# A hybrid retention and RG-LRU layer on one core: the order of instructions planned from a draft of the program, instead of by priorities

## The chip, the cores and the metric

The kernel runs on one core of a Trainium2 chip. The metric is the time of one execution on the device in microseconds (us), the median over several runs. Engines are named as in the profile: PE is TensorE (PEld its weight loads), DVE is VectorE, ACT is ScalarE, POOL is GpSimd, SP is SyncE, which here issues nearly all DMAs. Each engine takes its instructions in the one order that was fixed when the program was built.

## What is computed

One layer of a streaming encoder on 1024 positions of width 1024, in float32. The reference, cut to what matters here:

```python
h = rms_norm(x, norm1_w[l])
proj = h @ w_in[l]
q, k, v, g_ret, x_lru, y_lru, gate_ret, gate_lru = jnp.split(proj, SPLIT_POINTS, axis=-1)
...
o = chunkwise_retention(q, k, v.reshape(bsz, seq, RET_HEADS, RET_DV))
o = head_group_norm(o, ret_gn_w[l])
y_a = (o * jax.nn.silu(g_ret.astype(jnp.float32))).astype(x.dtype) @ w_ret_o[l]
xc = causal_depthwise_conv(x_lru, lru_conv_w[l], lru_conv_b[l])
hl = rg_lru(xc, lru_w_r[l], lru_b_r[l], lru_w_i[l], lru_b_i[l], lru_lambda[l])
y_b = (hl * jax.nn.gelu(y_lru.astype(jnp.float32))).astype(x.dtype) @ w_lru_o[l]
mix = (jax.nn.sigmoid(gate_ret + merge_gate_b[l, 0]) * y_a
       + jax.nn.sigmoid(gate_lru + merge_gate_b[l, 1]) * y_b)
x = x + mix @ w_out[l]
h = rms_norm(x, norm2_w[l])
up = h @ ffn_w_up[l]
gate, val = jnp.split(up, [D_FF], axis=-1)
gate = causal_depthwise_conv(gate, ffn_conv_w[l], ffn_conv_b[l])
x = x + (jax.nn.gelu(gate) * val) @ ffn_w_down[l]
return rms_norm(x, norm_f_w)
```

## The kernel before

**Matrix products.** Every large product is done in fp32r with a split of both operands into a high part and a rest: `split` copies a tile to fp32r on ACT (a CAST) and subtracts it on DVE, and three matmuls (`PASSES`) stand for one product. A `Job` is one piece of weights (256 columns, or 128 and 128) against all positions; its four weight blocks come by DMA (`loads`), and are split ahead (`preps`, driven by `pump`). Most jobs are `fast`: `mm_fast` does one level of Strassen's scheme, seven products of twelve matmuls instead of eight. It holds its sums in three PSUM banks; `keep` copies a bank to SBUF on ACT, `total` adds a bank to such a copy on DVE, and the bank is then used for another product. A late `keep` or `total` therefore stops PE at the next matmul into that bank. The right-hand operands are split into `hi` and `lo` by `operand`, `tsets` and `kept_sums`, generators that `build` drives between products.

**Buffers.** `Units` hands out numbered buffers of 128x512: `u` (81 in SBUF, for operands and everything else), `w` (22 in SBUF, for weights), `g` (6 PSUM banks for the large products) and `a` (2 PSUM banks for all small work). A name such as `g5_461` is bank 5 in its 461st use.

**Stages.** The jobs of the input projection come first (0 to about 770 us); `retention_head`, `ret_out` and `lru_block` run between them as generators that `advance` steps. In the retention (about 150 to 430 us) each block has three small steps that depend on each other: a product of 128 columns, a DVE multiplication with a mask, and products of 256 columns. In `lru_block` (about 440 to 720 us) a convolution on DVE and ACT gives two tiles, which are split; for each of two gates and two halves six small matmuls go to one of the two `a` banks, and an ACT sigmoid empties it. Then come the output projections of both branches, `w_out`, the norm, the up projection (about 970 to 1380 us) and three parts of the down projection, whose last one writes the output.

**What sets the order.** The Tile layer schedules the traced program by priorities: an instruction's place in the source sets its priority, and `tc.high_priority(offset)` moves it forward. `hp()` wraps the weight splits, `SOON` (400) the operand builders, `NOW` (3000) the copies and sums that empty a bank and what a job emits, and `OLD` (800) the last steps of the up projection. `Tap` records the last instruction of DVE and ACT, and `Behind` adds an edge without a semaphore, so that the operand splits that are issued through `BS` and `BV` do not stand before the last bank copy on their engine. As `Tap` and `Behind` issue the instructions, most DVE and ACT work has line L136 (`Tap`) or L153 (`Behind`) in the profile.

Of the kernel before, what the change touches and what calls it, by code (L numbers as in the profile page):

```python
# [125 lines left out]
class Tap:  # L126


    def __init__(self, eng):
        self.eng, self.last = eng, None  # L130

    def __getattr__(self, name):
        fn = getattr(self.eng, name)

        def call(*args, **kw):
            ins = fn(*args, **kw)  # L136
            self.last = ins.ins.name
            return ins
        return call


class Behind:


    def __init__(self, tc, eng):
        self.tc, self.eng, self.last = tc, eng, None
        self.how = mybir.DependencyInfo(mybir.DependencyClass.NoSync, mybir.DependencyReason.DATA)

    def __getattr__(self, name):
        fn = getattr(self.eng, name)  # L150

        def call(*args, **kw):
            ins = fn(*args, **kw)  # L153
            if self.last is not None:
                self.tc.add_manual_dep(ins.ins, self.last, self.how, reason="behind the banks' copies")
            return ins
        return call
# [12 lines left out]
NOW, SOON, OLD = 3000, 400, 800  # L170
# [10 lines left out]
def tile_trunk_layer(ctx, tc, x, xt, positions, params, consts, normf, w_in, w_ro, w_lo,  # L181
                     w_out, w_up, w_dn, w_gate, out):
    nc = tc.nc
    V, S, G, PE, SY = Tap(nc.vector), Tap(nc.scalar), nc.gpsimd, nc.tensor, nc.sync
# [32 lines left out]
    def hp(offset=1500):  # L217
        return tc.high_priority(offset=offset)

    def split(src, get=get, S=S, V=V):  # L220

        hi, lo = get(F32R), get(F32R)
        S.copy(hi, src)
        V.tensor_sub(lo, src, hi.bitcast(F32))
        return hi, lo

    BS, BV = Behind(tc, nc.scalar), Behind(tc, nc.vector)
# [28 lines left out]
    state = {"load": None, "prep": None, "blocks": 0, "raws": 0, "hp": False, "ff": 0, "reserve": RESERVE, "force": False}  # L258
# [77 lines left out]
    def pump(force=None):  # L336
        with (hp() if state["hp"] else nullcontext()):
            while force is not None and force[1] not in force[0].blk:
                assert next(state["prep"]) is not None
            while state["blocks"] < NBLK and len(W) >= 4:  # L340
                if next(state["prep"]) is None:
                    break
            while state["raws"] < AHEAD and len(W) >= 4 and W.free():
# [56 lines left out]
    def emit(jb, m, h, src, unit):  # L400
# [4 lines left out]
        if V.last != v:  # L405
            BV.last = V.last
# [1248 lines left out]
```

## Time and profile before

| what | value |
|---|---|
| median of 3 runs | 1633.09 us (1632.9 to 1635.78) |
| the profiled execution | 1634.66 us, its span (first to last instruction) 1632.8 us |
| granted TensorE clock, mean | 0.998 |
| busy DVE, ACT, POOL | 1322.2, 908.7, 46.3 us |
| bytes moved by DMA | 271.09 MB, 166 GB/s over the span |

In a row of the timeline the first number is the start in us from the start of the span, the second the time from the start of the row's first instruction to the end of its last. Brackets hold the idle time of that engine before the row and what ended it. In a row of windows stand the stretch and its length, and then the busy time of each engine with the number of instructions that began in it. A matmul is counted as busy to its modelled end, and matmuls overlap, so their spacing is less than their mean duration.

### The profile page before, as it was taken

How to read it: one execution, taken by the hardware profiler on the slowest of the kernel's cores; microseconds unless marked ns; L12 is line 12 of the kernel's file. 1: busy time of each engine (PE TensorE's matmuls, PEld its weight loads, DVE VectorE, ACT ScalarE, POOL GpSimd, SP SyncE). 2: the span in 40 equal slices, each digit the busy share in tenths (PEclk: the TensorE clock that was granted, in tenths of full speed). 3: DMA queues.
4: the chain of work that ended last, by engine and by line, in shares of the span. 5: the costliest groups of instructions: out<-in, count | busy, mean ns of one | idle time of the engine just before them, and what ended most of it. 6: DMA issues, size and time to landing. Idle time of an engine off the chain costs nothing.

```text
span 1632.8 us, 21508 instructions
## 1 busy us (share of the span) xinstructions
PE 1611.5 (99%) x7176; PEld 1317.7 (81%) x7176; DVE 1322.2 (81%) x2393; ACT 908.7 (56%) x1535; POOL 46.3 (3%) x68
## 2 busy tenths in 40 slices
PE   9999999999999999999999999999999999999998
PEld 7788888888887878778878778888888888888876
DVE  8998768686888888968879799777777778887885
ACT  7574544435477879863345675444444446463653
POOL 0001000000000000000000001000000000000000
PEclk9999999999999999999999999999999999999999
DMA  8253324142433437667797335444444456877751
GB/s 294 71 181 103 114 74 142 52 136 68 136 113 104 136 97 243 225 202 246 246 300 257 106 123 194 135 136 136 136 141 142 149 167 214 292 252 260 258 191 67
DMA packets 151439, 271.09 MB, mean 166 GB/s; under 512 B 16800, under 2 KB 25120, under 8 KB 151328
## 3 DMA queue, kind: packets, MB, share of 16 engines
q1 hardware_dynamic: 145664, 253.63, 48.4%
q0 software_dynamic: 4224, 13.64, 2.6%
q10 hardware_dynamic: 1440, 2.46, 0.4%
q8 instruction: 56, 0.92, 0.2%
q14 instruction: 55, 0.45, 0.1%
HBM read 188.92 MB, written 75.50 MB: 162 GB/s over the span
## 4 chain that ended last, share of the span: by engine, by line
PE 57%; DVE 6%; ACT 3%; issue 1%; DMA 1%; POOLq 0%; POOL 0%; DVEq 0%; ACTq 0%; SPq 0%
PE g L519 47%; PE g L464 8%; DVE u L136 3%; PE a L932 2%; DVE w L136 2%; ACT u L136 1%; DVE u L153 1%; ACT L136 1%; PE a L1394 0%; ACT w L136 0%; DMA w<-mix_d 0%; DMA x_d<-u 0%; DMA u<-x_d 0%; ACT u L153 0%; ACT a L136 0%
## 5 line engine op out<-in xcount | busy, mean ns | idle before, releaser
L519 PE MATMUL g<-u,w 128*128 128x512 f32 x5544 | 1295.6, 393 | 5.7 <-ACT u L136 3.1
L519 PEld LDWEIGHTS g<-u,w 128*128 128x128 f32 x5544 | 1036.5, 188 | 224.2 <-ACT u L136 7.4
L136 DVE TENSOR_TENSOR w<-w,w 128x512 fp32r<-128x512 f32 (+1 forms) x766 | 519.3, 687 | 74.4 <-ACT w L136 49.6
L136 ACT CAST w<-w 128x512 fp32r<-128x512 f32 x502 | 309.9, 621 | 381.0 <-PE g L519 268.2
L136 DVE TENSOR_TENSOR u<-u,u 128x512 f32<-128x512 f32 (+1 forms) x411 | 278.7, 689 | 91.4 <-ACT u L136 65.6
L136 DVE TENSOR_TENSOR u<-g,u 128x512 f32<-128x512 f32 x260 | 178.6, 688 | 73.2 <-PE g L519 55.2
L136 ACT COPY u<-g 128x512 f32<-128x512 f32 x242 | 140.3, 581 | 132.5 <-PE g L519 123.8
L464 PE MATMUL g<-u,w 128*128 128x512 f32 x768 | 181.6, 392 | 0.0
L464 PEld LDWEIGHTS g<-u,w 128*128 128x128 f32 x768 | 143.3, 188 | 30.1 <-ACT u L136 0.8
L153 DVE TENSOR_TENSOR u<-u,u 128x512 fp32r<-128x512 f32 (+1 forms) x216 | 139.7, 689 | 1.5 <-ACT u L153 1.2
L136 DVE SCALAR_TENSOR_TENSOR u<-u,par,u 128x511 f32<-128x511 f32 (+4 forms) x220 | 133.9, 631 | 5.1 <-ACT u L136 4.4
L153 ACT CAST u<-u 128x512 fp32r<-128x512 f32 x184 | 104.5, 620 | 34.2 <-DVE u L153 14.4
L136 ACT ACTIVATE u<-u,par 128x512 f32<-128x512 f32 (+1 forms) x115 | 86.5, 772 | 47.7 <-DVE u L136 45.5
L136 ACT ACT_TABLE_LOAD x76 | 97.5, 1283 | 3.0 <-PEq L1647 1.7
L1445 POOL DMA_DIRECT2D ff_d<-u x48 | 36.1, 752 | 1222.5 <-DVE u L136 1210.7
L136 ACT ACTIVATE u<-u 128x512 f32<-128x512 f32 x98 | 61.6, 633 | 15.4 <-DVE u L136 15.1
L932 PE MATMUL a<-u,u 128*128 128x512 f32 x192 | 50.7, 400 | 3.7 <-ACT u L136 2.0
L136 ACT ACTIVATE u<-a,par 128x512 f32<-128x512 f32 (+1 forms) x64 | 41.6, 688 | 12.5 <-PE a L932 7.8
L932 PEld LDWEIGHTS a<-u,u 128*128 128x128 f32 x192 | 34.6, 188 | 15.9 <-ACT u L136 5.7
L136 DVE SCALAR_TENSOR_TENSOR u<-u,u 128x512 f32<-128x512 f32 x46 | 31.5, 689 | 9.7 <-ACT u L136 9.2
L136 ACT ACTIVATE a<-u 128x512 f32<-128x512 f32 x40 | 24.0, 599 | 26.9 <-DVE u L136 24.4
L136 ACT COPY u<-a 128x256 f32<-128x256 f32 (+1 forms) x34 | 13.1, 385 | 36.2 <-PE a L1045 33.6
(80 smaller groups left out, 514.1 us busy)
## 6 DMA issues: line engine op xcount, KB each, us to landing
w<-w_in SPq DMA_DIRECT2D x112, 256.0 KB, 2.7
w<-w_up SPq DMA_DIRECT2D x96, 256.0 KB, 2.7
u<-w_dn SPq DMA_DIRECT2D x88, 256.0 KB, 3.2
u<-x_d SPq DMA_DIRECT2D x60, 256.0 KB, 3.9
x_d<-u SPq DMA_DIRECT2D x48, 256.0 KB, 3.3
ff_d<-u POOLq DMA_DIRECT2D x48, 256.0 KB, 3.1
td_d<-u SPq DMA_DIRECT2D x48, 256.0 KB, 3.3
w<-ff_d SPq DMA_DIRECT2D x48, 256.0 KB, 3.7
```

The costliest lines, as they stand in the source:

```text
L136: ins = fn(*args, **kw)
L153: ins = fn(*args, **kw)
L464: PE.matmul(banks[m, h], jb.blk[an][a][:, c], o[b], start=left[m, h] == 2 and n == 0, stop=left[m, h] == 1 and n == 11)
L519: PE.matmul(bank, w[a][:, c], need(op, (bn, j))[b], start=first and n == 0, stop=n == 11, skip_group_check=True)
L932: PE.matmul(ps, wg[g][a][:, cs], xs[k][b], start=q == 0, stop=q == 5)
L1445: G.dma_start(ff_d[g, 4 * h:4 * h + 4, kh, :, kk, :].rearrange("t p c -> p t c"), c.rearrange("p (t c) -> p t c", t=4))
```

## The change

The classes `Tap` and `Behind` and all uses of `tc.high_priority` are taken out. In their place the program is built twice. The first build is a draft. `Plan` reads its instructions and dependencies (those through released buffers too), gives each a duration by a formula, works backwards from the end to the latest start of each (`latest`, with PE in the draft's order at first), and then forwards (`forward`): on each engine, of the instructions that are ready, the one with the earliest deadline is taken next. Small matmuls into the `a` banks go before all others. A consumer of a DMA is held back by another 1500 ns, and a matmul behind another engine's work by 400 ns. ACT puts off work that needs another function table, within limits, and SP issues a DMA only when the modelled backlog allows it. This is done twice, the second time with PE's new order. The second build has the same instructions (one table load on ACT fewer, 75), and `Plan.chain` ties each instruction to the one before it on its engine by an edge without a semaphore. Jobs, buffers and all numbers that set sizes stay.

```diff
+class Step:
...
+        if self.eng == "PE":
+            if self.flip:
+                t = 108.5
+            elif any("float32r" in s[3] for s in self.ins):
+                t = 226.6
...
+            self.hold, self.tail = t, 163.0
+        elif self.eng == "DVE":
+            slow, quick = 68 + n / 0.96, 68 + n / 1.92
...
+            self.hold, self.tail = t, 87.0
+        elif self.eng == "Activation":
+            if self.op == "TensorCopy":
+                t = (50 if bank else 95) + n / 1.2
...
+class Plan:
...
+    SWITCH, CHAIN, HAND = 1283.0, 35.0, 45.0
+    READ, WRITE, MOVE, QUEUE = 1900.0, 1500.0, 800.0 / 262144, 500.0
+    LATE_DMA, LATE_PE, BACKLOG, KEEP = 1500.0, 400.0, 300.0, 2000.0
...
+    def chain(tc, nc, order):
+        how = mybir.DependencyInfo(mybir.DependencyClass.NoSync, mybir.DependencyReason.DATA)
+        by = {i.name: i for i in nc.cur_bb.bb.instructions}
+        for names in order.values():
+            for a, b in zip(names, names[1:]):
+                tc.add_manual_dep(by[b], a, how, reason="the plan's order")
...
+    def lag(self, a, b, late=True):
+
+        if a.dma:
+            return self.HAND + self.LATE_DMA * late
+        if a.eng == b.eng:
+            return self.CHAIN if a.eng in ("DVE", "Activation", "Pool") else None
+        return self.HAND + self.LATE_PE * (late and b.eng == "PE")
...
+    def order(self, rounds=2):
+        pe = [n for n, s in self.steps.items() if s.eng == "PE"]
+        for _ in range(rounds):
+            start = self.latest(pe)
+            span = -min(start[n] for n in pe)
+            rank = {n: t + span - (1e7 if self.steps[n].small else 0.0) for n, t in start.items()}
+            order, _ = self.forward(rank)
+            pe = order["PE"]
+        return order
...
-NOW, SOON, OLD = 3000, 400, 800
...
-    V, S, G, PE, SY = Tap(nc.vector), Tap(nc.scalar), nc.gpsimd, nc.tensor, nc.sync
+    V, S, G, PE, SY = nc.vector, nc.scalar, nc.gpsimd, nc.tensor, nc.sync
...
         def keep(bank):
             u = get()
-            with hp(NOW):
-                BS.last = S.copy(u, bank).ins.name
+            S.copy(u, bank)
             return u
...
         def total(u, bank, m, c):
-            with hp(NOW):
-                BV.last = V.tensor_add(u, bank, u).ins.name
-            emit(jb, m, c, u, u)
+            V.tensor_add(u, bank, u)
+            jb.emit(m, c, u, u)
...
-            op[key] = split(t, get, BS, BV)
+            op[key] = split(t)
...
+    draft, steps = build()
+    nc, _ = build(Plan(steps, draft).order())
     r = run_bass_kernel_spmd(nc, [arrays], core_ids=[0])
```

Three places show what the plan moves. **ACT, the first operand splits of the retention's output projection**, near 830 us. `u1_1331` and `u68_1387` are two bank copies of `keep`, `w15_1308` is a weight block's cast, the other casts are operand splits. Before:

```order
L136 COPY u1_1331_7728<-g0_229_7613 128x512
L136 CAST w15_1308_7869<-w20_1307_7867 128x512
L153 CAST u23_1342_7746<-u49_1315_7700 128x512
L153 CAST u52_1346_7752<-u5_1316_7702 128x512
L153 CAST u3_1350_7758<-u11_1317_7704 128x512
L153 CAST u36_1354_7764<-u9_1318_7706 128x512
L153 CAST u46_1358_7770<-u48_1319_7708 128x512
L153 CAST u25_1375_7796<-u29_1320_7710 128x512
L153 CAST u17_1379_7802<-u33_1321_7712 128x512
L153 CAST u34_1383_7808<-u26_1322_7714 128x512
L136 COPY u68_1387_7814<-g0_229_7613 128x512
```

Now:

```order
L719 COPY u1_1331_7728<-g0_229_7613 128x512
L424 CAST u34_1383_7808<-u26_1322_7714 128x512
L424 CAST u59_1401_7836<-u38_1345_7750 128x512
L424 CAST u53_1404_7840<-u10_1349_7756 128x512
L424 CAST u44_1407_7844<-u30_1353_7762 128x512
L424 CAST u47_1410_7848<-u12_1357_7768 128x512
L424 CAST w15_1308_7869<-w20_1307_7867 128x512
L424 CAST u9_1426_7906<-u16_1378_7800 128x512
L424 CAST u18_1432_7914<-u57_1386_7812 128x512
L424 CAST u28_1429_7910<-u40_1382_7806 128x512
L719 COPY u68_1387_7814<-g0_229_7613 128x512
```

Between the weight block's cast and the second copy stood eight casts, and now stand three; five stand between the first copy and the weight block's cast, where none stood.

**PE, a block of `lru_block`**, near 613 us. `a1_337` and `a0_339` are the two gates' banks of one half, `a1_341` the first of the next, `g` are the large products. Before:

```order
L932 MATMUL a1_337_5696<-u76_756_5670,u61_738_5538 128x512
L932 MATMUL a0_339_5705<-u76_756_5670,u4_742_5561 128x512
L519 MATMUL g2_165_5622<-u80_170_367,w12_986_5556 128x512
L932 MATMUL a1_337_5696<-u35_757_5671,u61_738_5538 128x512
L932 MATMUL a1_337_5696<-u76_756_5670,u5_739_5539 128x512
L932 MATMUL a0_339_5705<-u35_757_5671,u4_742_5561 128x512
L932 MATMUL a0_339_5705<-u76_756_5670,u62_743_5562 128x512
L519 MATMUL g2_165_5622<-u8_173_372,w3_985_5555 128x512
L519 MATMUL g2_165_5622<-u1_174_373,w3_985_5555 128x512
L932 MATMUL a1_341_5736<-u33_749_5610,u61_738_5538 128x512
```

Now (the first of these rows stands 84 matmuls sooner on PE):

```order
L1115 MATMUL a1_337_5696<-u76_756_5670,u61_738_5538 128x512
L1115 MATMUL a0_339_5705<-u76_756_5670,u4_742_5561 128x512
L705 MATMUL g0_159_5436<-u80_170_367,w5_948_5371 128x512
L705 MATMUL g0_159_5436<-u8_173_372,w4_947_5370 128x512
L705 MATMUL g0_159_5436<-u1_174_373,w4_947_5370 128x512
L1115 MATMUL a1_337_5696<-u35_757_5671,u61_738_5538 128x512
L1115 MATMUL a1_337_5696<-u76_756_5670,u5_739_5539 128x512
L1115 MATMUL a0_339_5705<-u35_757_5671,u4_742_5561 128x512
L1115 MATMUL a0_339_5705<-u76_756_5670,u62_743_5562 128x512
L705 MATMUL g0_159_5436<-u8_173_372,w5_948_5371 128x512
```

The rest of the split (`u35_757`, from DVE) is used three large matmuls behind its high part, where it was one. Ten large matmuls now follow before the first one into `a1_341`, where there were two.

**DVE, the last part of the down projection**, near 1565 us. `u8_2822 <- g5_461` is the `total` that frees bank 5. Before:

```order
L153 TENSOR_TENSOR u14_2800_14653<-u16_2760_14565,u28_2799_14652 128x512
L153 TENSOR_TENSOR u10_2803_14657<-u40_2764_14571,u61_2802_14656 128x512
L153 TENSOR_TENSOR u43_2806_14661<-u58_2768_14577,u23_2805_14660 128x512
L136 TENSOR_TENSOR w18_2675_14784<-w17_2639_14559,w9_2674_14783 128x512
L153 TENSOR_TENSOR u25_2811_14687<-u80_2782_14605,u7_2810_14686 128x512
L136 TENSOR_TENSOR w20_2692_14867<-w12_2671_14769,w8_2677_14787 128x512
L136 TENSOR_TENSOR w5_2681_14807<-w16_2654_14680,w3_2680_14806 128x512
L153 TENSOR_TENSOR u48_2814_14691<-u45_2786_14611,u9_2813_14690 128x512
L136 TENSOR_TENSOR u8_2822_14757<-u8_2822_14757,u44_2818_14714 128x512
L136 TENSOR_TENSOR u49_2816_14711<-u49_2816_14711,u2_2827_14791 128x512
L136 TENSOR_TENSOR u8_2822_14757<-g5_461_14633,u8_2822_14757 128x512
```

Now:

```order
L729 TENSOR_TENSOR u52_2808_14664<-g1_460_14632,u52_2808_14664 128x512
L1733 TENSOR_TENSOR u63_2819_14733<-u52_2808_14664,u27_2797_14627 128x512
L1740 TENSOR_SCALAR nst_76<-nst_76 128x1
L725 TENSOR_TENSOR u8_2822_14757<-u8_2822_14757,u44_2818_14714 128x512
L425 TENSOR_TENSOR w18_2675_14784<-w17_2639_14559,w9_2674_14783 128x512
L729 TENSOR_TENSOR u8_2822_14757<-g5_461_14633,u8_2822_14757 128x512
```

Between the sum from `g1_460` and this `total` stood thirteen rows, and now stand four. Five operand rests (`u14_2800` to `u48_2814`), one sum (`u49_2816`) and one weight rest above the piece shown (`w21_2668`) have gone ahead of the sum from `g1_460`, and two weight rests behind the `total`. On PE the next product into bank 5 comes five matmuls sooner.

306 lines of the change are left out of this document (224 added, 82 removed).

## The prediction

> **What bounds the kernel now.** I read the page first, then who waited for whom on PE, then stretches of the span, then the timeline where PE waited longest.
>
> ```profile
> PE 1611.5 (99%) x7176; PEld 1317.7 (81%) x7176; DVE 1322.2 (81%) x2393; ACT 908.7 (56%) x1535; POOL 46.3 (3%) x68
> L519 PE MATMUL g<-u,w 128*128 128x512 f32 x5544 | 1295.6, 393 | 5.7 <-ACT u L136 3.1
> ...
> L136 ACT COPY u<-g 128x512 f32<-128x512 f32 x242 | 140.3, 581 | 132.5 <-PE g L519 123.8
> ```
>
> PE is busy for all but 21.3 us of the 1632.8, so no order of instructions can save more than a per cent or so. The change leaves every matmul in; it can only take away time in which PE waits, or add some.
>
> ```profile
> 1000.00:1360.00 360.00, 360.00 (x1590) 298.18 (x1590) 275.67 (x456) 170.19 (x284) 28.53 (x38) 1.00 0.47 147
> ...
> 1624.75 0.84 PE L519 MATMUL g<-u,w 128*128 128x512 f32 x3
> ```
>
> From 1000 to 1360 us PE never stops: 360/1590 = 226.4 ns from one matmul to the next. The mean duration of 393 ns contains 167 ns in which the next already runs, so a wait costs its idle time and some 0.17 us more. PE's last matmul ends at 1625.6; the 7.2 us behind it are the output's tail, and the first matmul begins at 1.2. That leaves 12.9 us of idle time between, and these waits are nearly all of it:
>
> ```profile
> PE g L519 <- ACT u L136: 3.1, 3, 2.2
> PE g L519 <- DVE u L136: 2.5, 2, 1.8
> PE a L932 <- ACT u L136: 2.0, 3, 0.9
> PE a L932 <- DVE u L136: 1.6, 3, 0.9
> PE g L495 <- DVE u L136: 1.4, 2, 0.7
> PE a L1286 <- DVE st L136: 1.2, 1, 1.2
> PE g L424 <- ACT u L136: 1.0, 1, 1.0
> PE a L1394 <- ACT a L136: 0.4, 1, 0.4
> PE a L1043 <- DVE sm L136: 0.3, 1, 0.3
> PE a L1004 <- DVE u L136: 0.2, 1, 0.2
> ```
>
> Without the one at the very start (L1286) they are 18 waits and 12.5 us, 0.69 us each; with 0.17 us for each, 15.6 us. PE waits for ACT and DVE alone, never for a DMA directly, and DVE, the busier of the two, is idle for 19% of the span: PE waits where a bank copy or a rest stands in the wrong place of a queue.
>
> **The change part by part.** No instruction is added or dropped but one table load on ACT. What moves is costed place by place.
>
> *The bank copy at 830 us (the ACT order shown above).*
>
> ```profile
> 828.07 0.62 ACT L136 CAST w<-w 128x512 fp32r<-128x512 f32 x1 [2.65 <-DMA w<-mix_d]
> 828.60 4.26 ACT L153 CAST u<-u 128x512 fp32r<-128x512 f32 x8
> 832.76 0.57 ACT L136 COPY u<-g 128x512 f32<-128x512 f32 x1
> ...
> 823.73 6.51 PE L519 MATMUL g<-u,w 128*128 128x512 f32 x28
> 830.08 1.07 PE L464 MATMUL g<-u,w 128*128 128x512 f32 x4
> 833.39 0.97 PE L519 MATMUL g<-u,w 128*128 128x512 f32 x3 [2.24 <-ACT u L136]
> ```
>
> ACT idles 2.65 us for a weight block's DMA with operand casts behind it. Then it runs eight of them, (4.26-0.62)/7 = 0.52 us apart. The bank was complete at 823.73+6.51 = 830.24, its copy begins at 832.76, and PE idles 2.24 us. In the new order five casts (2.6 us) stand ahead of the weight block's, which fills the 2.65; three stand behind it, done by 828.6+1.56 = 830.2, just as the bank is complete. The copy ends by 830.9. PE has six matmuls of another bank there where it had four, until 830.08+6x0.226 = 831.4. So the wait goes: 2.24+0.17 = 2.4 us. Bounds 0 and 2.4; I take 2.4.
>
> *The bank copy at 43 us.*
>
> ```profile
> 43.82 0.59 ACT L136 COPY u<-g 128x512 f32<-128x512 f32 x1 [1.50 <-DVE nst L136]
> ...
> 44.46 1.88 PE L424 MATMUL g<-u,w 128*128 128x512 f32 x7 [1.02 <-ACT u L136]
> ```
>
> The bank copied here was complete before 20 us; the copy was only late in its queue. It now stands 16 rows sooner on ACT, and PE asks for the bank ten matmuls sooner (2.3 us), which 16 rows of some 0.5 us each more than cover. 1.02+0.17 = 1.2 us; bounds 0 and 1.2, and I take 1.2.
>
> *The LRU blocks (the PE order shown above).*
>
> ```profile
> 500.00:740.00 240.00, 236.30 (x1029) 191.55 (x1029) 204.55 (x346) 179.85 (x260) 0.00 (x0) 1.00 0.52 171
> ...
> 608.56 0.72 PE L932 MATMUL a<-u,u 128*128 128x512 f32 x2 [0.81 <-ACT u L136]
> ...
> 607.89 0.62 ACT L136 CAST u<-u 128x512 fp32r<-128x512 f32 x1 [0.59 <-DVE u L136]
> ...
> 614.54 1.26 ACT L136 ACTIVATE u<-a,par 128x512 f32<-128x512 f32 x2 [1.03 <-PE a L932]
> ```
>
> In these 240 us PE begins 1029 matmuls, worth 1029x0.2264 = 233.0 us, so 7.0 us are lost. The six L932 waits are 3.6+6x0.17 = 4.6 of them; the rest lies in shorter waits. The cause is distance. One large matmul (0.23 us) stood between the use of a split's high part and of its rest, though DVE needs about 0.7 us for the rest. Two (0.45 us) stood before a bank that two sigmoids (1.26 us) had yet to empty. Now it is three (0.68 us) and ten (2.26 us). What waits at 608.56 is the head of the chain: convolution, cast, matmul. That matmul now stands 84 to 92 places sooner, 19 to 21 us, so convolution and cast must come that much sooner too; ACT has 60 us of idle time in the stage and DVE 35 to fit them in. The distances repair most, the head of the chain may still be late once a block: I take 5.0 of the 7.0, bounds 0 and 7.0.
>
> *The total at 1565 us (the DVE order shown above).*
>
> ```profile
> 1564.00:1570.00 6.00, 4.16 (x12) 3.02 (x12) 5.80 (x12) 1.79 (x5) 1.32 (x1) 0.74 0.53 185
> ...
> 1544.19 0.69 DVE L136 TENSOR_TENSOR w<-w,w 128x512 f32<-128x512 f32 x1 [1.65 <-DMA w<-ff_d]
> ...
> 1549.67 0.69 DVE L136 TENSOR_TENSOR u<-g,u 128x512 f32<-128x512 f32 x1 [1.17 <-DMA u<-x_d]
> ...
> 1557.49 1.28 DVE L136 TENSOR_TENSOR u<-g,u 128x512 f32<-128x512 f32 x2
> 1566.72 3.66 PE L519 MATMUL g<-u,w 128*128 128x512 f32 x8 [1.84 <-DVE u L136]
> ```
>
> PE idles 1.84 us, and then the granted clock drops: eight matmuls take 3.66 us where 8x0.226+0.17 = 2.0 would do, 1.7 us more. In all 1.84+0.17+1.7 = 3.7. DVE instructions follow each other 0.6 us apart (1.28 less 0.69). The sum from `g1_460` is the second of the pair at 1557.49, so it begins at 1558.1; four rows (1.9 us) behind it the total would now begin at 1560.6 and end by 1561.3. Seven rows have gone ahead of that sum, though, 4.2 us of DVE work; if nothing hides them the total ends at 1565.5, and PE, which asks for the bank five matmuls sooner, at 1563.6, still waits 1.9 us. DVE idles 1.65+1.17 = 2.8 us shortly before; if the moved rows fill that, 1.4 us are left and the total ends at 1562.7, in time. Bounds 0 and 3.7; I take 3.7, by the rows that are idle.
>
> [...]
>
> *What else moves.* At the start ACT's cast of the first weight block now stands behind the first scaling of x, which waits for its DMA:
>
> ```profile
> 3.88 0.62 ACT L136 CAST w<-w 128x512 fp32r<-128x512 f32 x1 [0.71 <-DMA w<-w_in]
> ...
> 6.53 1.33 ACT L136 ACTIVATE u<-u,par 128x512 f32<-128x512 f32 x2 [2.03 <-DMA u<-xt]
> ...
> 8.34 11.97 PE L495 MATMUL g<-u,w 128*128 128x512 f32 x51 [0.70 <-DVE u L136]
> ```
>
> So it begins at about 7.15 and not at 3.88, which puts the first product back by some 0.66 us, and takes the second one's wait of 0.70 away, as the rest it waits for now comes first on DVE: 0, bounds -0.7 and +0.7. The other L519 waits (3.1+2.5-2.24-1.84 = 1.5 us) I leave: the last bank's at the end has the same order as before, and where the other waits for DVE the total stands two rows sooner (1.2 us) and PE eight matmuls sooner (1.8 us). In the retention the steps now lie 5 to 7 large matmuls apart, where they lay 3 to 10; L1043 waited 0.3 us in all: 0.
>
> *New waits.* The plan holds a matmul back by 0.4 us behind its producer; where the chip is later than that, PE stops. The trace before cannot show such waits. The lower bound is none, the upper one as many as now, 18 of 0.69+0.17 us, 15.5 us. I take three, 2.6 us: nearest to none, since the reserve is more than half a wait.
>
> The sum: -2.4-1.2-5.0-3.7+2.6 = -9.7 us. The profiled execution took 1634.66 us (span 1632.8 and 1.9 around it), 1.6 above the median of 1633.09. Nothing around the span changes, so I take the 9.7 off the median: 1623.4, **predicted 1623 us**.
>
> **The rivals.**
>
> *Slower: a row brought forward holds up the bank copies.* Each engine's order is fixed, and the old rule that bank copies go first is gone. A cast brought forward whose DMA is late now stands ahead of a copy, and PE stops at the bank. For it: at 828.07 ACT stood 2.65 us behind one late DMA, and such loads take long to land:
>
> ```profile
> u<-td_d SPq DMA_DIRECT2D x48, 256.0 KB, 5.4
> ```
>
> Against it: the plan keeps 1.5 us in reserve behind each landing, and what it brings forward had landed well before. One such place costs what 830 us costs today, 2.4 us. The new order is slower by over 3.3 us once six of the 242 copies are held up like that (9.7+3.3 = 13.0 = 5.4x2.4); with nine it is 9x2.4-9.7 = +11.9, 1645 us. [...]
>
> *No change: the waits only move.* Where DVE is full, PE is bound by its work, which stays the same:
>
> ```profile
> 40.00:120.00 80.00, 78.98 (x345) 64.14 (x344) 78.71 (x183) 55.22 (x88) 0.00 (x0) 1.00 0.39 127
> 640.00:680.00 40.00, 39.12 (x172) 31.79 (x171) 39.11 (x73) 30.68 (x48) 0.00 (x0) 1.00 0.77 260
> ```
>
> There DVE works 98% of the time. If the LRU blocks' waits come from that, their 5.0 us stay, and with some four new waits more (3.5 us) the gain is 1.2: 1632 us. Against it: over the whole 500 to 740 us DVE is busy for 204.55 of 240.
>
> *All of it.* No new waits, the LRU blocks lose nothing, and the small waits left go too: 2.4+1.2+7.0+3.7+1.5 = 15.8, 1617 us. For it: there is idle time on both engines beside every wait. Against: the order at the very end is unchanged.
>
> That the order does not change at all is excluded by the pieces shown.
>
> **How the numbers follow.** Forecast (1618 to 1629): 0.54; all of it: 0.18; no change: 0.10; slower: 0.18. A measurement of this kernel cannot tell less than 0.2%, 3.3 us, from no change. Faster 0.54+0.18 = 0.72, same 0.10, slower 0.18. Alone the forecast would have a range of 1618 to 1629. The range that holds eight in ten reaches below the whole gain, to 1615, and up to where the rival of late copies has lost 5 us, 1638; beyond lie about 0.06 and 0.10.
>
> **What would show it.** Right: PE idle time between first and last matmul falls from 12.9 to about 5 us; no wait of L519's successor over 1 us near 830 and 1565 us, and no loss of clock there; 500 to 740 us holds about 1050 matmuls; 1000 to 1360 us stays without a gap. Wrong: waits of PE for bank copies or totals at places that had none (the slower rival), or the same idle time at other lines (no change). If PE's waits fall and the time does not, the tail or the start has grown.

## The result, and the profile after

| | before | after |
|---|---|---|
| median, us | 1633.12 (1632.9 to 1635.78) | 1614.44 (1613.97 to 1614.62) |
| ratio | | 0.9882, 95% interval 0.9864 to 0.9899 |
| the profiled execution, us | 1634.66, span 1632.8 | 1613.97, span 1612.2 |

The change makes the kernel 18.7 us faster; 9.7 were forecast, and the median lies 0.6 us below the low end of the range. The first view is the page of the changed kernel, busy times by engine, and then who waited for whom on PE (in all, times, longest).

```profile
PE 1599.3 (99%) x7176; PEld 1320.5 (82%) x7176; DVE 1320.6 (82%) x2393; ACT 908.2 (56%) x1534; POOL 45.8 (3%) x68
```

```profile
PE a L1187 <- DVE u L1179: 1.7, 1, 1.7
PE g L681 <- ACT w L424: 1.5, 1, 1.5
PE a L1469 <- DVE heat L1449: 1.4, 1, 1.4
PE g L705 <- ACT u L719: 0.7, 1, 0.7
PE a L1115 <- ACT u L424: 0.4, 2, 0.2
```

Of the waits of the list before three are left: the start (L1469 stands in place of L1286), the last bank's 0.7 us, and 0.4 us of the LRU blocks' 3.6 (L1115 stands in place of L932). Two waits are longer, 1.7 us at L1187 (0.2 us at L1004 before) and 1.5 at L681, the first product. PE is idle for 1612.2-1599.3 = 12.9 us, of which 1.4 lie ahead of its first matmul and 7.1 behind its last: 4.4 between, where there were 12.9. The idle time fell by 8.5 us and the span by 20.6. So most of the gain was never idle time of PE. The next view is stretches of the changed kernel.

```profile
150.00:430.00 280.00, 280.00 (x1346) 234.29 (x1345) 212.35 (x474) 131.03 (x235) 0.00 (x0) 1.00 0.33 102
500.00:740.00 240.00, 239.61 (x1054) 197.10 (x1053) 204.13 (x348) 171.60 (x254) 0.00 (x0) 1.00 0.56 183
810.00:834.00 24.00, 24.00 (x108) 19.87 (x107) 22.45 (x37) 15.43 (x28) 0.00 (x0) 1.00 0.99 334
850.00:960.00 110.00, 110.00 (x517) 91.17 (x516) 92.06 (x175) 70.94 (x136) 0.79 (x1) 1.00 0.45 150
1000.00:1340.00 340.00, 340.00 (x1502) 281.62 (x1501) 259.22 (x428) 162.60 (x270) 27.04 (x36) 1.00 0.47 145
1540.00:1560.00 20.00, 20.00 (x90) 16.56 (x89) 16.54 (x31) 11.07 (x23) 1.54 (x2) 1.00 0.65 216
```

The places of 830 and 1565 us, now some 11 and 20 us earlier, run without a gap. The two of these stretches that the prediction did not show read in the kernel before:

```profile
150.00:430.00 280.00, 279.48 (x1337) 229.98 (x1335) 205.73 (x452) 130.39 (x232) 0.00 (x0) 1.00 0.33 99
850.00:960.00 110.00, 109.47 (x506) 87.86 (x505) 93.36 (x176) 71.22 (x139) 0.79 (x1) 1.00 0.55 181
```

PE was "busy" there for all but 0.52 and 0.53 us, and yet in the same length 9 and 11 matmuls fewer began (a row of the trace each; an f32 product stands as two: L1038 has 64 rows for 32 products). A matmul is counted busy to its modelled end; one that starts up to 0.17 us late (393 ns of mean duration less 226.4 ns of spacing) leaves no gap. The lateness does stand in the trace, in the waits of the weight loads (PEld). The same list for PEld, kernel before, first between 150 and 430 us, then between 850 and 1000:

```profile
PEld a L1038 <- ACT u L136: 2.6, 12, 0.2
PEld a L1043 <- issue: 1.6, 4, 0.7
PEld a L1104 <- PE g L519: 1.3, 4, 0.4
PEld a L1004 <- DVE u L136: 1.0, 2, 0.6
PEld a L1043 <- DVE sm L136: 0.9, 2, 0.5
PEld a L1043 <- ACT w L136: 0.7, 4, 0.2
```

```profile
PEld a L1394 <- ACT a L136: 1.7, 4, 0.9
PEld g L519 <- ACT u L136: 1.5, 4, 0.6
PEld a L1394 <- DVE u L136: 0.8, 2, 0.5
...
```

The first list sums to 8.1 us; the second goes on with waits of 0.8 us and less. The lists of the changed kernel are empty for both stretches.

To see the whole, I took from the trace when each matmul began, and subtracted from its distance to the next the spacing that this kind of matmul has where nothing hinders it (among them 226.6 ns for 512 columns in fp32r, 427 ns for the twelve warm-up matmuls on `heat`, 108.5 ns for a transposition of 128x128, 217 and 430.5 ns for f32 products of 128 and 256 columns, each two rows of the trace; medians of the trace). What is left is **PE's lost time**. It is 31.0 us before and 10.3 after, 20.7 us less, which is the difference of the spans (20.6). (The medians differ by 18.7, since the profiled execution was 1.5 us above its median before and 0.5 below it after.) By stages, named by their times in the kernel before:

| stage, us | before | after | gained | forecast |
|---|---|---|---|---|
| 0-100 (start, bank copy at 43) | 3.6 | 1.2 | 2.4 | 1.2 |
| 100-150 | 0.0 | 2.3 | -2.3 | -2.6 (three new waits, anywhere) |
| 150-450 (retention) | 6.1 | 2.7 | 3.4 | 0 |
| 450-750 (LRU blocks) | 7.5 | 2.4 | 5.1 | 5.0 |
| 750-850 (bank copy at 830) | 2.7 | 0.0 | 2.7 | 2.4 |
| 850-1000 (norm) | 4.1 | 0.6 | 3.5 | 0 |
| 1000-1530 (1420 and 1488) | 1.8 | 0.1 | 1.7 | 0 |
| 1530-1580 (total at 1565) | 4.0 | 0.0 | 4.0 | 3.7 |
| the end | 1.0 | 1.0 | 0 | 0 |

### The profile page after: what moved, and what is told of

It reads as the page before. It is cut to its first block, busy times and chain, and to the rows that moved or that the text cites. A ratio compares the mean times of both kernels' runs of the same rounds, so it can differ in the third digit from the quotient of the medians.

```text
span 1612.2 us, 21662 instructions
## 1 busy us (share of the span) xinstructions
PE 1599.3 (99%) x7176; PEld 1320.5 (82%) x7176; DVE 1320.6 (82%) x2393; ACT 908.2 (56%) x1534; POOL 45.8 (3%) x68
## 4 chain that ended last, share of the span: by engine, by line
PE 61%; DVE 2%; ACT 2%; issue 1%; POOLq 0%; POOL 0%; DVEq 0%; ACTq 0%
PE g L705 50%; PE g L650 10%; DVE u L1097 1%; PE a L1115 1%; DVE u L425 0%; PE a L1577 0%; ACT u L1118 0%; DVE w L425 0%; ACT L1118 0%; ACT L1138 0%; DVE u L729 0%; ACT u L424 0%; ACT u L1126 0%; DVE u L1058 0%; ACT L1304 0%
## 5 line engine op out<-in xcount | busy, mean ns | idle before, releaser
L425 DVE TENSOR_TENSOR w<-w,w 128x512 fp32r<-128x512 f32 x502 | 342.0, 685 | 91.0 <-ACT w L424 86.8
L729 DVE TENSOR_TENSOR u<-g,u 128x512 f32<-128x512 f32 x198 | 135.7, 687 | 78.3 <-PE g L705 58.9
L424 ACT CAST u<-u 128x512 fp32r<-128x512 f32 x224 | 132.0, 620 | 70.4 <-PE g L705 12.4
L719 ACT COPY u<-g 128x512 f32<-128x512 f32 x198 | 114.9, 580 | 76.4 <-PE g L705 74.9
L425 DVE TENSOR_TENSOR u<-u,u 128x512 fp32r<-128x512 f32 x224 | 146.5, 684 | 4.8 <-ACT u L424 4.5
L1623 DVE SCALAR_TENSOR_TENSOR u<-u,par,u 128x511 f32<-128x511 f32 (+1 forms) x96 | 71.4, 745 | 3.9 <-ACT u L1620 3.5
L1115 PE MATMUL a<-u,u 128*128 128x512 f32 x192 | 50.4, 394 | 0.6 <-ACT u L424 0.4
L1620 ACT ACTIVATE u<-u,par 128x512 f32<-128x512 f32 x48 | 39.3, 818 | 15.4 <-DVE u L729 15.0
L513 DVE TENSOR_TENSOR w<-w,w 128x512 f32<-128x512 f32 x66 | 45.3, 687 | 1.2
L519 DVE TENSOR_TENSOR w<-w,w 128x512 f32<-128x512 f32 x66 | 45.3, 686 | 0.5
L526 DVE TENSOR_TENSOR w<-w,w 128x512 f32<-128x512 f32 x66 | 45.3, 686 | 0.4
L510 DVE TENSOR_TENSOR w<-w,w 128x512 f32<-128x512 f32 x66 | 45.2, 685 | 0.5 <-DMA w<-w_up 0.4
L725 DVE TENSOR_TENSOR u<-u,u 128x512 f32<-128x512 f32 x42 | 28.8, 687 | 19.9 <-ACT u L719 19.8
L1115 PEld LDWEIGHTS a<-u,u 128*128 128x128 f32 x192 | 35.2, 188 | 10.4 <-ACT u L424 1.8
L1627 DVE TENSOR_TENSOR u<-u,u 128x512 f32<-128x512 f32 x48 | 33.0, 687 | 5.8 <-ACT u L1626 5.7
L1097 DVE SCALAR_TENSOR_TENSOR u<-u,par,u 128x511 f32<-128x511 f32 (+2 forms) x48 | 35.4, 744 | 0.0
```

What stands on the lines that cost most here:

```text
L513: V.tensor_sub(s1, s1, a11)
L519: V.tensor_sub(a11, a21, a11)
L526: V.tensor_sub(s1, a12, s1)
L719: S.copy(u, bank)
L729: V.tensor_add(u, bank, u)
L1097: V.scalar_tensor_tensor(c[:, s:], src[:, :TH - s], w, c[:, s:], ALU.mult, ALU.add)
```

## The experiments

Unless said otherwise each is the changed source with one edit. Several hold engines to the order of the kernel before: `OLD` holds that order of instruction names for the engines named, an edge in the plan ties each to the next, and the rest is planned around it.

```diff
+        self.tied = set()
+        for eng, text in OLD:
+            row = ["I-%d" % k for k in np.frombuffer(zlib.decompress(base64.b64decode(text)), np.uint16)]
+            row = [n for n in row if n in self.steps]
+            for a, b in zip(row, row[1:]):
+                if a not in self.before[b]:
+                    self.before[b].append(a)
+                    self.after[a].append(b)
+                    self.tied.add((a, b))
...
     def lag(self, a, b, late=True):
+        if (a.name, b.name) in self.tied:
+            return None
```

All results together, first the ratio to the kernel before with its interval, then PE's lost time of the profiled execution, whole and by stage:

| run | median us | ratio | lost | 0-150 | 150-450 | 450-750 | 750-850 | 850-1000 | 1000-1580 |
|---|---|---|---|---|---|---|---|---|---|
| before | 1633.1 | | 31.0 | 3.6 | 6.1 | 7.5 | 2.7 | 4.1 | 5.8 |
| after | 1614.4 | 0.9882 (0.9864 to 0.9899) | 10.3 | 3.5 | 2.7 | 2.4 | 0.0 | 0.6 | 0.1 |
| e1_pe_sp_old | 1625.5 | 0.9942 (0.9927 to 0.9957) | 20.7 | 3.9 | 7.4 | 2.3 | 0.1 | 4.9 | 1.1 |
| e2_helpers_old | 1632.6 | 0.9985 (0.9975 to 0.9994) | 28.5 | 3.4 | 3.8 | 8.9 | 0.0 | 11.4 | 0.1 |
| e3_draft | 1642.6 | 1.0045 (1.0030 to 1.0059) | 32.4 | 2.9 | 5.8 | 6.0 | 2.5 | 3.3 | 10.9 |
| e4_no_reserve | 1625.2 | 0.9943 (0.9927 to 0.9958) | 22.8 | 7.0 | 6.0 | 2.6 | 0.8 | 1.2 | 4.2 |
| e5_all_old | 1635.5 | 1.0009 (0.9996 to 1.0021) | 32.3 | 6.7 | 6.4 | 8.7 | 1.2 | 4.1 | 4.2 |
| e6_act_old | 1617.3 | 0.9898 (0.9883 to 0.9912) | 14.0 | 1.7 | 3.1 | 1.6 | 0.0 | 6.4 | 0.1 |
| e7_dve_old | 1634.2 | 0.9997 (0.9988 to 1.0006) | 30.5 | 5.3 | 2.9 | 5.0 | 2.0 | 13.4 | 0.4 |
| e10_dve_lru_old | 1624.3 | 0.9947 (0.9933 to 0.9960) | 18.8 | 8.3 | 2.7 | 5.7 | 0.0 | 0.9 | 0.1 |
| e8_no_small_first | 1613.2 | 0.9883 (0.9869 to 0.9896) | 9.3 | 3.7 | 2.8 | 1.0 | 0.0 | 0.6 | 0.1 |
| e9_late_1500_800 | 1624.0 | 0.9940 (0.9925 to 0.9955) | 20.7 | 14.5 | 3.1 | 0.3 | 0.0 | 1.7 | 0.1 |
| e11_dma_2500 | 1624.6 | 0.9951 (0.9937 to 0.9964) | 21.2 | 15.6 | 2.6 | 1.1 | 0.0 | 0.6 | 0.1 |
| e12_reserves_sp | 1626.6 | 0.9959 (0.9946 to 0.9971) | 23.1 | 16.2 | 3.2 | 0.4 | 0.2 | 2.0 | 0.1 |
| e13_halves | 1612.3 | 0.9866 (0.9845 to 0.9888) | 8.8 | 2.0 | 2.7 | 2.3 | 0.0 | 0.6 | 0.1 |
| e14_halves_2500 | 1616.1 | 0.9892 (0.9873 to 0.9912) | 12.2 | 6.8 | 2.5 | 1.1 | 0.0 | 0.6 | 0.1 |
| e15_halves_800 | 1611.5 | 0.9862 (0.9844 to 0.9880) | 7.7 | 1.6 | 3.0 | 0.3 | 0.0 | 1.7 | 0.1 |
| e16_halves_deadline | 1609.3 | 0.9848 (0.9830 to 0.9867) | 5.4 | 1.1 | 2.6 | 0.1 | 0.0 | 0.4 | 0.1 |

The end loses 1.0 in every run but e7 (1.3). In e5, which repeats the order of before, single stages differ from it by up to 3 us and the whole by 1.3, so one stage of one execution is sure to some 3 us at 0-150 and to some 1.5 us elsewhere. The kernel before was run beside each group of runs, with medians from 1632.8 to 1635.4 us; so the ratios are what compares runs, and a difference of two medians is sure to some 2 us.

### Which engine's order carries the gain

**e1_pe_sp_old.** PE and SP in the old order, ACT and DVE planned.

```diff
+OLD = [("PE", "..."), ("SP", "...")]
```

> PE and the DMA queue of SP keep the order of the kernel before; ACT and DVE (and POOL) are planned around it. Between PE's first and last matmul the kernel before lost 31.0 us against the matmuls' own spacing and the changed one 10.3. Of the 31.0 lay 9.2 at large products that waited for a bank copy or a total (1.2 at 43, 2.5 at 830, 1.6 at 1420 and 1488, 3.9 at 1565 us), and 15.9 in the three stages with small matmuls (6.1 in 150-450, 7.7 in 450-750, 4.1 in 850-1000, of which 2 us are the cost of the small matmuls themselves). Theory queues (the gain is made on ACT and DVE, whatever PE's order): nearly all of the gain is here, 1614 to 1618 us. Theory spacing (the stages with small matmuls gain by the distance that PE's own order gives them, the large products by ACT and DVE): only the 9.2 us come, 1633.1-9.2 = 1624 us, and 450-750 us loses about 7 us as before.

Measured 1625.5: by the time, the theory of spacing. By the stages it is half right. The waits for bank copies and totals are gone, and the retention (7.4) and the norm (4.9) stay as bad as before; but the LRU blocks lose 2.3 us, with PE in the very order that lost 7.5. The stretch of that run, to be read beside 1029 matmuls before and 1054 after:

```profile
500.00:740.00 240.00, 239.27 (x1053) 197.16 (x1053) 211.83 (x358) 186.34 (x268) 0.00 (x0) 1.00 0.52 172
```

The retention's loss also shows in its list of PE's waits (`sm` is the masked product that DVE writes):

```profile
PE a L1246 <- DVE sm L1243: 2.0, 4, 0.7
```

**e2_helpers_old.** ACT and DVE in the old order, PE and SP planned.

```diff
+OLD = [("DVE", "..."), ("Activation", "...")]
```

> The reverse: ACT and DVE keep the order of the kernel before, PE, SP and POOL are planned around it. Theory spacing: the small matmuls gain, the waits for copies and totals stay: 1633.1-12 = 1621 us, with the waits near 830 and 1565 us still there. Theory queues: PE's order alone gains little, 1630 to 1633 us. A third theory, that the plan is worth something only as a whole (small matmuls brought forward on PE wait for casts that the old queues of ACT and DVE bring late): slower than before, above 1636 us.

Measured 1632.6: the new orders of PE, SP and POOL alone are worth 0.15%, as the theory of queues has it. They mend the retention (3.8) and, unforeseen, also the waits for copies and totals (0.0 and 0.1); PE's order was planned around the old queues here, and that it asks for those banks later is the likely reason. The LRU blocks lose 8.9 us and the norm 11.4. But the small matmuls of the LRU blocks (L1135 here, L932 in the kernel before) hardly wait any more; what PE waits for there is a bank copy at 640 us, 3.4 us, with a granted clock of 0.68 and 29 matmuls from 640 to 650 us behind it:

```profile
PE g L725 <- ACT u L739: 5.3, 5, 3.4
...
PE a L1135 <- DVE u L445: 0.3, 1, 0.3
```

So the copies and totals can be mended from either side, the retention from PE's (SP's old order leaves it mended in the next two runs), the small matmuls of the LRU blocks again from either side, while the LRU stage as a whole needs the new queues, and the norm both.

**e6_act_old** and **e7_dve_old** part the two queues.

```diff
+OLD = [("Activation", "..."), ("SP", "...")]   # e6
+OLD = [("DVE", "..."), ("SP", "...")]          # e7
```

> ACT and SP keep the order of before; PE, DVE and POOL are planned around them. With PE's old order and ACT and DVE planned, PE lost only 2.3 us in the LRU stage (450 to 750 us) where before lost 7.5, and with ACT and DVE old and PE planned 8.9: what repairs this stage is the order on ACT and DVE. Theory DVE (convolution and rests stand behind operand rests in DVE's queue): the LRU stage loses about 2.5 us here, and the time is 1614 plus the norm's share, up to 1620 us. Theory ACT (casts and sigmoids stand behind weight and operand casts): the stage loses 7 to 9 us, and the time is 1622 to 1626 us.

> The reverse: DVE and SP keep the order of before; PE, ACT and POOL are planned around them. Theory DVE: the LRU stage loses 7 to 9 us, and the time is 1625 to 1632 us. Theory ACT: it loses about 2.5 us, and the time is 1615 to 1620 us. If both runs lose 4 to 5 us there, the old orders of both engines do harm.

Measured 1617.3 and 1634.2. ACT's and SP's old orders together cost 2.9 us, DVE's and SP's the whole gain. In the LRU blocks it is 1.6 against 5.0, as the theory DVE has it, though 5.0 is less than the 7 to 9 named, and the mechanism is not the theory's: 4.8 of the 5.0 lie at large products. The larger loss of e7 lies in the norm, 13.4 us, for which no size had been named.

**e10_dve_lru_old.** Only the 431 DVE instructions of 440 to 740 us in the old order.

```diff
+OLD = [("DVE", "...")]   # 431 names
```

> Planned as the changed kernel, but the 431 DVE instructions that ran between 440 and 740 us in the kernel before keep their order of then. With the whole of DVE old the run took 1634 us, with ACT and SP old only 1617. Theory DVE in the LRU stage: PE's loss between 450 and 750 us rises from 2.4 us to 5 to 9, the other stages stay, and the time is 1614.4 plus 3 to 7, 1617 to 1621 us. Rival (what was lost with the whole of DVE old lay in the norm, 850 to 1000 us, where that run lost 13.4): the LRU stage loses under 4 us here and the time is within 2 us of 1614.

The LRU blocks lose 5.7 us, the norm 0.9: DVE's order inside this stage costs 3.3 us there. The time, 1624.3, lies above the 1621 named, because the first 150 us lost 4.8 us more, for the reason found below (SP stood 10.9 us for a buffer). The losses do not come back where they were; the largest single one, 3.3 us, is a product of the output projection that waits for an operand rest:

```profile
649.66 1.29 DVE L444 TENSOR_TENSOR u<-u,u 128x512 fp32r<-128x512 f32 x2
...
650.40 1.87 PE L669 MATMUL g<-u,w 128*128 128x512 f32 x7 [3.14 <-DVE u L444]
```

Parted by what PE was late with, the lost time of this stage (450 to 750 us) reads:

| run | old order on | small matmuls | large products |
|---|---|---|---|
| before | all | 6.9 | 0.6 |
| after | none | 2.2 | 0.2 |
| e1 | PE, SP | 0.7 | 1.6 |
| e6 | ACT, SP | 0.6 | 0.9 |
| e2 | ACT, DVE | 1.0 | 7.8 |
| e7 | DVE, SP | 0.2 | 4.8 |
| e10 | DVE, in this stage | 0.1 | 5.6 |

With either PE or the queues planned the small matmuls lose 1.0 us or less (2.2 with both). DVE's old order brings another loss in their place, most of it between 638 and 651 us, where PE stands for bank copies (e2, e7) and for an operand rest (e10). Why these come late there was not tested.

**e3_draft** and **e5_all_old** ask whether it is the plan at all.

```diff
-    nc, _ = build(Plan(steps, draft).order())
+    nc, _ = build()                           # e3
...
+OLD = [...]                                   # e5: all five engines
```

> The draft itself is run: the changed source without priorities and without the plan, ordered by the place in the source alone. If it is the removal of the priorities that helps, it lies between 1614 and 1625 us. If the plan does it, the draft is slower than the kernel before, since its bank copies and totals stand in the order of the source behind the operand casts: at 2.4 us for each copy that is late (the one at 830 us before) and some 20 of 242 late, 1680 us; anything above 1640 us fits.

> The changed source, chained on all five engines to the order that the kernel before had. If the order alone carries the gain, this is the kernel before in another writing: 1633 us, with the same 31 us lost on PE at the same places. If the chain or the missing priorities themselves save something (fewer semaphores, say), it is faster than before by over 0.2%, below 1630 us.

e5 is the kernel before within its interval: the chain and the missing priorities are worth nothing by themselves, the order is all. e3 is 0.45% slower than before: taking the priorities away does not help. (Its profiled execution was the fastest of nine, 1636.5 us, so its lost time is on the low side.) My price for it was far off, however. Not some 20 copies stopped PE but seven, the largest losses being 3.8, 2.3 and 2.1 us.

### The reserves

**e4_no_reserve, e9_late_1500_800, e11_dma_2500, e12_reserves_sp** change what the plan holds back; **e8_no_small_first** drops a rule, with SP tied to its order in the changed kernel.

```diff
-    LATE_DMA, LATE_PE, BACKLOG, KEEP = 1500.0, 400.0, 300.0, 2000.0
+    LATE_DMA, LATE_PE, BACKLOG, KEEP = 0.0, 0.0, 300.0, 2000.0       # e4
+    LATE_DMA, LATE_PE, BACKLOG, KEEP = 1500.0, 800.0, 300.0, 2000.0  # e9
+    LATE_DMA, LATE_PE, BACKLOG, KEEP = 2500.0, 400.0, 300.0, 2000.0  # e11, with rounds=3
+    LATE_DMA, LATE_PE, BACKLOG, KEEP = 2500.0, 600.0, 300.0, 2000.0  # e12, with rounds=3
...
-            self.hold = 750.0 if self.eng == "Pool" else 330.0
+            self.hold = 750.0 if self.eng == "Pool" else 450.0           # e12
...
-            rank = {n: t + span - (1e7 if self.steps[n].small else 0.0) for n, t in start.items()}
+            rank = {n: t + span for n, t in start.items()}           # e8
```

> The changed kernel planned without its reserves (no 400 ns behind another engine's work for a matmul, no 1500 ns behind a DMA). If the reserves are what keeps new waits of PE few: waits of some tenths of a us at many small matmuls, 1614.4 plus 5 to 10 us, 1619 to 1625 us. If the order by deadlines alone does it, 1614.4 within 2 us.

> The changed kernel planned with 800 ns in place of 400 behind another engine's work for a matmul. Without the reserves the run was 10.7 us slower than the changed kernel. If 400 ns is still too short in places, the waits of 0.3 to 0.4 us left in the LRU stage (464, 581 and 673 us) go: 1613 us, and the wait of 1.9 us at 139 us stays, since it is for a DMA. If 400 ns covers what the chip is late by, more of it only pushes small matmuls later and brings waits elsewhere: 1616 to 1622 us.

> The changed kernel planned without the rule that small matmuls go before all others on PE, with SP's order held as it is in the changed kernel; 251 rows of PE and 796 of DVE move against it. If the rule carries the gain in the retention and the LRU stage, PE loses several us more there: 1618 to 1625 us. If order by deadline is enough, 1614.4 within 2 us.

> The changed kernel planned with 2500 ns in place of 1500 behind a DMA, and three rounds in place of two. If the wait of 1.9 us at 139 us comes from the short reserve behind SP's DMAs, it goes and nothing else changes: 1612.5 us. If a longer reserve brings waits at other places, as 800 ns behind another engine did at 46 us, 1615 to 1624 us.

> The changed kernel planned with 450 ns for a DMA issue of SP in place of 330 (its issues follow each other 0.42 us apart at the closest tenth in the changed kernel's trace), 2500 ns behind a DMA, 600 ns for a matmul behind another engine, and three rounds. If the waits left in the changed kernel come from a model that is too hopeful, those at 139, 464, 581 and 673 us go (1.9+0.3+0.4+0.3): 1611.5 us. If they are chance, others take their place: 1614 to 1620 us.

e4: the reserves are worth 10.7 us, more than half the gain. Without them the retention loses 6.0 as before, and the large products wait again for eight bank copies. Not all of the price is the reserves' own: 3.5 us of it lie ahead of 150 us, where the wait at L1187 has grown to 2.5 us; in the changed kernel that wait comes from a dependency that the plan did not see (next section). e8: 1613.2, the small-first rule carries nothing. e9, e11 and e12 came out at 1624 to 1627, above both theories of each (e11 by 0.6 us only): behind 150 us they lose 5.4 to 6.9 us, the changed kernel 6.8 (in the LRU blocks e9 loses 0.3 against 2.4), but 14 to 16 us go ahead of it. The next rows are of e9: a line of the waits of SP's queue, then ACT and PE in order of time.

```profile
SPq L987 <- PE g L610: 16.2, 1, 16.2
...
```

```profile
50.32 1.36 ACT L424 CAST w<-w 128x512 fp32r<-128x512 f32 x2 [9.37 <-DMA w<-w_in]
...
55.77 2.08 PE L932 MATMUL a<-u,ones 128*128 128x512 f32 x2 [8.72 <-DVE u L927]
```

SP stood 16.2 us at a load of `positions` (L987), because the buffer was still read by PE. The weight loads behind it came late, ACT and DVE stood 9.4 us for them, then PE 8.7. To stand there is not what costs: the changed kernel stands 12.7 us at the same load, and PE loses nothing by it. What differs is how many loads of `w_in` SP issued ahead of it. They are 11 in e9, e10, e11 and e12, which lose 8.3 to 16.2 us before 150 us, and 12 or 13 in all others, which lose 7.0 at most. This is no reserve that is too short.

### The dependency that the plan did not see

The load at L987 is one of two that fill the two halves of one tile. In the draft's dependencies only the first of the two waits for the buffer's last readers; the second is held by standing behind it on the same queue. The plan knew only the dependencies, took the second half as free, and put it first; on the chip it waits for the readers all the same (12.7 us in the changed kernel, until PE's L610 is done). The rotary step's swaps of halves (L1175, L1176) are such pairs too, and in the changed kernel all 16 of SP's stand the wrong way round. From them comes its wait at L1187. The rows are SP's waits between 120 and 140 us, and then the timeline of the changed kernel:

```profile
SPq L1176 <- DMA sg_d<-u: 3.3, 1, 3.3
```

```profile
138.56 0.69 DVE L1178 TENSOR_TENSOR u<-u,u 128x512 f32<-128x512 f32 x1 [2.02 <-DMA u<-u]
...
141.12 0.66 PE L1187 MATMUL a<-cst,u 128*128 128x128 f32 x4 [1.72 <-DVE u L1179]
```

SP stands 3.3 us for a buffer that a store still reads, the swaps behind it are late, DVE waits 2.0 us for one, and PE 1.7 for DVE. The repair lets the second DMA into a tile wait for what the first waits for:

```diff
+        last = {}
+        for n, s in self.steps.items():
+            key = s.eng, s.outs[0][0]
+            a = last.get(key)
+            last[key] = n
+            if a is None or a in self.before[n] or key[1].split("_")[0] in DRAM or not s.dma:
+                continue
+            for b in self.before[a]:
+                if b not in self.before[n]:
+                    self.before[n].append(b)
+                    self.after[b].append(n)
```

e13 has only this; e14 has it with e11's edit, e15 with e9's, and e16 with e11's and e8's rank, without SP tied.

> The changed kernel, whose plan now lets the second of two DMAs into one tile wait for what the first waits for; 19 rows of SP and 11 of PE move. Theory hidden dependency: the wait of 1.9 us at 139 us goes and nothing comes in its place, 1614.4-2 = 1612.5 us. Theory short reserve: the wait stays, 1614.4 us.

> The kernel with 2500 ns behind a DMA and three rounds, with the same repair. Without it the run took 1624.6 us, with 11.0 us lost before 100 us and 4.6 between 100 and 150. Theory hidden dependency: these go down to about 1.2 and 0.3, 1624.6-14 = 1610.5 us. Theory short reserve (or a longer reserve does harm by itself): it stays above 1618 us.

> The kernel with 800 ns for a matmul behind another engine's work, with the same repair. Without it 1624.0 us, with 12.8 lost before 100 us and 1.7 between 100 and 150. Theory hidden dependency: 1624.0-13 = 1611 us. Otherwise above 1618 us.

> The repair, 2500 ns behind a DMA, three rounds, and no rule of small matmuls first: on PE too the earliest deadline goes first. If that rule is of no use, as its removal with SP's order held showed, this is the fastest of all, 1609 to 1611 us. If it guards the stages with small matmuls, PE loses several us between 150 and 450 or 450 and 750 us: 1614 to 1620 us.

e13: 1612.3, as the hidden dependency has it; the wait at L1187 falls from 1.7 to 0.7 us. e15: 1611.5 against 1624.0 without the repair. SP still stands at the load of `positions` in both, 12.7 and 10.4 us, but the twelfth weight load is ahead of it. e14: 1616.1, between the two theories; the 10 us at the start come back, but 5.8 us stay between 100 and 150, where PE waits 2.9 us for a total:

```profile
128.66 0.69 DVE L1057 TENSOR_TENSOR u<-u,u 128x512 f32<-128x512 f32 x1 [6.17 <-issue]
...
132.42 1.12 PE L716 MATMUL g<-u,w 128*128 128x512 f32 x2 [2.90 <-DVE u L740]
```

DVE stood 6.2 us ahead of L1057, for which the profile names no releaser. L1057 reads tiles that POOL's DMAs swap, issued from 123.2 to 126.8 us; that it waited for them is likely and was not tested. e16 is the fastest of all, 1609.3 us, 5 us below the changed kernel. It differs from e14 only by the rule of small matmuls first, and without that rule the 5.8 us are not there. The list of PE's waits of e16 is shown whole:

```profile
PE a L1480 <- DVE heat L1460: 1.4, 1, 1.4
PE g L716 <- ACT u L730: 0.7, 1, 0.7
PE g L692 <- ACT w L435: 0.4, 1, 0.4
```

## Why the prediction was wrong

- **The budget of lost time: the step that failed.** "These waits are nearly all of it": 18 waits, 12.5 us idle, 15.6 us with the overlap. PE lost 31.0 us, and e16 shows that all but 5.4 can be had. I counted matmuls against their spacing in one stage with waits only, 500 to 740 us, and there it gave 7.0 us where the idle waits gave 4.6. In the retention I wrote "L1043 waited 0.3 us in all: 0", and the norm had no term; there the loss was in late weight loads: between 150 and 430 us PEld waited 8.1 us and PE was idle for 0.52. The busy times of the stage say the same: from 150 to 430 us PE's busy time rose by 0.52 us, that of PEld from 229.98 to 234.29. Over the whole span PEld tells little, 81% before and 82% after. The retention and the norm gained 3.4 and 3.5 us of the 10.8 by which the profiled executions beat the forecast sum (20.5 by the stages, against 9.7). The waits that I left standing at 1420 and 1488 us gave 1.7, and the first 100 us gave 1.2 beyond the copy at 43 us, most of it at the start; the sizes of the other terms make up 1.0.
- **830, 43 and 1565 us.** Taken at 2.4, 1.2 and 3.7; the stage at 830 gained 2.7, the place at 43 us 1.2 (of the 2.4 of 0-100), the stage at 1565 4.0. Right, and for 1565 the idle rows on DVE did hide the moved ones. But the new order of ACT's and DVE's queues, on which I argued, was not the only way to it: in e2, with these two old, the new order of PE and SP removes the same waits.
- **The LRU blocks.** Taken at 5.0, measured 5.1. "The cause is distance" is half of it. With the new distances on PE and ACT's and DVE's old orders (e2) the small matmuls lose 1.0 us where they lost 6.9; but with the old distances and the new queues (e1) they lose 0.7, so either repairs them. What the sum did not hold is that with DVE's old order PE then stands at large products instead, and the stage loses 5.0 to 8.9 us (e2, e7, e10). That is the rival of no change, the waits only move, and DVE's new order kept it away. That 5.0 was met so closely is luck.
- **The retention.** Here it is PE's order, for which I had taken nothing: PE old 7.4, PE planned 2.5 to 3.8, except without reserves (6.0). That distance is what counts in it is likely from that exception, since the reserves are what keeps a matmul away from its producer.
- **New waits.** 2.6 us for three were taken, and one of 1.9 came (2.3 in its stage); the size was met by luck. I laid them to a reserve of 0.4 us that is too short; the one that came was behind a load whose dependency the plan did not see, and e13 took most of it away. That the reserves matter was right, and e4 gives their price, 10.7 us at most.
- **The start.** Taken at nothing, since the first product was to begin 0.66 us later. The second one's wait is gone as forecast (0.94 lost before), but the first began at 7.14 us, where it began at 7.17. So the start gained some 0.9 us, a little more than its bound of 0.7. That the first product's wait reads longer (1.41 lost against 0.88) is because the last four of the twelve matmuls on `heat` ahead of it came 0.21 us apart in this execution, the others 0.43.
- **The rivals.** "All of it" came nearest (1617), and its sum had the same hole as mine, so the range ended too high. "Slower" had its mechanism right, a row brought forward that holds up what stands behind it: it came once in the changed kernel (1.9 us) and at 7 to 9 us in e9, e11 and e12. It was SP's queue that stood, for a buffer, not ACT's for a late landing.
- **The signs.** Idle time 4.4 us (about 5 forecast), 1054 matmuls in 500 to 740 us (about 1050), no gap in 1000 to 1340, no loss of clock at 1565: all as said, while the time missed. The idle time was the wrong thing to watch.

## What to carry to other kernels

PE was 99% busy here, stood idle for 12.9 us between its first and last matmul, and lost 31.0: count an engine's instructions per stretch against their unhindered spacing in every stage, and read the waits of the weight loads beside those of the matmuls (8.1 us against 0.5 in the retention). Whoever plans an order from a draft's dependencies must also take over what the draft's order held implicitly, above all on DMA queues: in e9 one load stood 16.2 us for a buffer, and SP issued nothing else until it went. The reserves behind DMAs and ahead of matmuls were worth up to 10.7 us here (e4), more than any one stage gained.

## What the runs showed of the hardware

In these runs the granted clock of PE did not fall at one length of wait. The rows are stretches behind places where PE lost 3.1 us (e14, at 132 us), 3.3 us (e10, at 650 us) and 1.6 us (e5, the same place as 1565 us in the kernel before, whose wait of 2.0 us cost 1.7 more, at 0.74 from 1564 to 1570 us).

The granted clock is the third number from the end of a row: 0.53, 1.00 and 1.00.

```profile
132.40:136.00 3.60, 3.58 (x9) 2.82 (x10) 3.51 (x11) 2.97 (x5) 0.00 (x0) 0.53 0.60 155
```

```profile
650.40:656.00 5.60, 5.60 (x24) 4.49 (x25) 5.60 (x10) 1.43 (x3) 0.00 (x0) 1.00 0.95 323
```

```profile
1569.60:1576.00 6.40, 6.29 (x28) 5.21 (x29) 4.71 (x11) 3.85 (x9) 2.06 (x2) 1.00 0.70 242
```

Over all 18 traces, behind the first 10 us, places where PE lost 1.5 to 2.5 us at once were followed by slow matmuls (427 ns apart in place of 227, as eight are from 1566.7 us on in the kernel before) in 2 cases of 18 (in one of them a second wait stood close behind), 2.5 to 3.4 us in 5 of 7, and over 3.5 us in 6 of 6, for 2.7 to 5.7 us each time. So 2.0 us was enough in the kernel before (0.74), and 3.3 us was not in e10 (1.00). What else the fall depends on was not shown.
